# The split of the weights into a rounded and a remaining part, in pieces of 512 instead of 256 elements

## The chip, the cores and the metric

The kernel runs on one core of one Trainium2 chip. The metric is device time in microseconds of one execution: the median of several runs. Of the core's engines this text speaks of PE (TensorE; PEld are its weight loads), DVE (VectorE), ACT (ScalarE), POOL (GpSimd) and SP (SyncE, which issues the DMAs).

## What is computed

One decoder layer for 512 tokens of width 1024, in float32:

```
u = rms_norm(x, norm_pre)
q_a, kv_a, g_a, z_a, qkv_b, z_b, merge = split(u @ w_in)
kc, vc = compress(kv_a[0]), compress(kv_a[1])        # small two-layer nets w1, w2 over blocks of 32
o_a = gated sum of compressed, selected and window attention (8 heads, 2 kv groups)
o_b = block-sparse attention (8 heads), which at 512 tokens is plain causal attention over two blocks of 256
y_a, y_b = o_a * silu(z_a), o_b * silu(z_b)
m = sigmoid(gate_a) * (y_a @ w_a) + sigmoid(gate_b) * (y_b @ w_b)
out = x + rms_norm(m @ w_o, norm_post)
```

All softmaxes carry a distance penalty.

## The kernel before

The matmuls take operands in a rounded 32-bit form (fp32r). To keep float32 precision the kernel writes each operand as a rounded part `hi` and the remaining part `lo`, and multiplies hi by hi, hi by lo and lo by hi (L168 to L170 in `proj`).

**Weights.** They come in 30 chunks of 128 x 2048 elements (1 MB), each loaded by SP into one of two `raw` buffers, then split on the chip in two slots of 1024 columns each; a slot has one of three `ws` buffers, which holds hi and lo. Splitting a slot is a list of pieces, and each piece is two instructions of the method `split_pieces`:

```
act.activation(hi, src, AF.Copy)                     # L115, ACT: the rounded part
dve.tensor_tensor(lo, src, f(hi), op=ALU.subtract)   # L116, DVE: what remains
```

Four functions say how a slot is cut: `std_pieces`, `pair_pieces` and `w1_pieces` cut it into four pieces of 256 elements per partition; `half_pieces(n)` into pieces of n elements, 256 for the chunks vb and 512 for the two chunks wo. So 28 chunks have 2 x 4 pieces of 256 (224 pieces), the last two chunks 2 x 2 pieces of 512 (8 pieces).

**Order.** `stream_gen` runs the chunks one after another: early chunks (kcvc, ksw, w1k, qa0, w1v, qa1), ten chunks that fill the attention phase (za, vb, zb, qkb), twelve of the merge (ga, gb, ab) and wo. While one slot is multiplied, after every step of the projection one piece of the next slot is issued. The last piece of a chunk's second slot calls `load_ahead`, which issues the load of a later chunk into the `raw` buffer that this sets free. In the attention phase `fill` interleaves the projection with the 24 attention units: scores (L928, L929), the addition of the bias with a running minimum on DVE (L932), the exponential on ACT (L934), scaling on DVE and POOL (L946), transposes on PE (L967), the split of the transposed probabilities on ACT (L968) and DVE (L969, which also frees the PSUM buffer for the next transposes), and the product with v (L987, L988).

At the start a block under `tc.manual_schedule()` writes the order out by hand; it holds the eight pieces of the first chunk, kcvc, as `first[0]` to `first[7]`. Behind it the framework's planner, with costs of its own, sets the order in which each engine gets its instructions: they need not stand in the order of the lines. On the chip each engine runs its list in that fixed order and waits at an instruction whose input or buffer is not ready.

The small net of the compression (L770 to L774 on ACT and DVE) is followed by a transpose on PE, `ph_k` or `ph_v` (L781), which stands in PE's list between matmuls of the chunk qa.

Of the kernel before, what the change touches and what calls it, by code (L numbers as in the profile page):

```python
# [41 lines left out]
def hybrid_block(ctx, tc, x, norm_pre, w_in, pe_k, w1_k, w2_k, pe_v, w1_v, w2_v,  # L42
# [21 lines left out]
    def ps(tag, name):  # L64
        return psum.tile([128, 512], F32, tag=tag, name=name)
# [54 lines left out]
    def std_pieces(s):  # L120

        def piece(k0):
            def fn(raw, slot):
                r = raw.rearrange("p (k c) -> p k c", k=8)[:, k0:k0 + 2, s * 128:(s + 1) * 128]
                v = slot.rearrange("p (h k c) -> p h k c", h=2, k=8)
                return r, v[:, 0, k0:k0 + 2], v[:, 1, k0:k0 + 2]
            return fn
        return [piece(k) for k in range(0, 8, 2)]

    def half_pieces(n):  # L130

        kk = 1024 // n
        def pieces(s):
            def piece(k):
                def fn(raw, slot):
                    r = raw.rearrange("p (k c) -> p k c", c=n)[:, s * kk + k]
                    v = slot.rearrange("p (h k c) -> p h k c", h=2, c=n)
                    return r, v[:, 0, k], v[:, 1, k]
                return fn
            return [piece(k) for k in range(kk)]  # L140
        return pieces

    def pair_pieces(s):

        def piece(k0):
            def fn(raw, slot):
                r = raw.rearrange("p (k g c) -> p k g c", k=8, g=2)[:, k0:k0 + 2, :, s * 64:(s + 1) * 64]
                v = slot.rearrange("p (h k g c) -> p h k g c", h=2, k=8, g=2)
                return r, v[:, 0, k0:k0 + 2], v[:, 1, k0:k0 + 2]
            return fn  # L150
        return [piece(k) for k in range(0, 8, 2)]

    def w1_pieces(s):
        def piece(k0):
            def fn(raw, slot):
                r = raw.rearrange("p (l e) -> p l e", l=16)[:, 8 * s + k0:8 * s + k0 + 2]
                v = slot.rearrange("p (l h e) -> p l h e", l=8, h=2)
                return r, v[:, k0:k0 + 2, 0], v[:, k0:k0 + 2, 1]
            return fn
        return [piece(k) for k in range(0, 8, 2)]  # L160

    def proj(slot, dst, kts=range(KT), rh=None, rl=None):

# [281 lines left out]
    def take_pieces(item):  # L445
        c, sl = item
        pieces = c.split_pieces(sl)

        def last(go=pieces[-1]):
            go()  # L450
            unsplit[c.name] -= 1
            if not unsplit[c.name]:
                del unsplit[c.name]
            load_ahead()
        return pieces[:-1] + [last]
# [92 lines left out]
    def x_stats(tt, parts=1):  # L548
        sq = s4.tile([128, D], F32, tag="s4", name=f"sq_{tt}")
        ss = early.tile([128, 2], F32, name=f"ss_{tt}")  # L550
        rs[tt] = early.tile([128, 1], F32, name=f"rs_{tt}")
        w = D // parts
        for n in range(parts):
            act.activation(sq[:, n * w:n * w + w], xt[tt][:, n * w:n * w + w], AF.Square, accum_out=ss[:, n:n + 1])
        sss[tt] = ss
        if parts == 2:
            r = rs[tt]
            dve.tensor_scalar(ss[:, 0:1], ss[:, 0:1], 1.0 / D, EPS, op0=ALU.mult, op1=ALU.add)
            dve.scalar_tensor_tensor(r, ss[:, 1:2], 1.0 / D, ss[:, 0:1], op0=ALU.mult, op1=ALU.add)
            pool.tensor_tensor(r, r, neghalf, op=ALU.pow)  # L560

    def x_stats_r(tt):
        rstd_of(sss[tt][:, 0:1], rs[tt], EPS)
# [3 lines left out]
    def x_diag(tt):  # L567
        diag[tt] = early.tile([128, 128], F32, name=f"diag_{tt}")
        dve.tensor_scalar(diag[tt], ident, rs[tt], None, op0=ALU.mult)

    def x_scale(tt, h):
        c = slice(512 * h, 512 * h + 512)
        act.activation(xt[tt][:, c], xt[tt][:, c], AF.Copy, scale=rs[tt])

    def x_transpose(tt, h):

        pt = ps("to"[h], f"ut_{tt}_{h}")
        for k in range(4):
            kk = 4 * h + k
            o, i = pt[:, k * 128:(k + 1) * 128], xt[tt][:, kk * 128:(kk + 1) * 128]  # L580
            if tt in diag:
                mm(o, i, diag[tt], start=True, stop=True)
            else:
                pe_eng.transpose(o, i, ident)
        up[tt, h] = pt

    def x_hi(tt, h):

        u = xt[tt][:, 512 * h:512 * h + 512].rearrange("p (k t) -> p k t", k=4)
        dve.tensor_tensor(u, up[tt, h].rearrange("p (k t) -> p k t", k=4),  # L590
                          npreT[:, 4 * h:4 * h + 4, None].to_broadcast([128, 4, 128]), op=ALU.mult)
        hi = uh[:, 4 * h:4 * h + 4, tt * 128:tt * 128 + 128]
        up[tt, h] = (u, hi)
        act.activation(hi, u, AF.Copy)

    def x_low(tt, h, eng=dve):
        u, hi = up[tt, h]
        eng.tensor_tensor(ul[:, 4 * h:4 * h + 4, tt * 128:tt * 128 + 128], u, f(hi), op=ALU.subtract)

    def wa_hi(k, eng=None):  # L600
        if eng is not None:
            eng.tensor_copy(wa_hl[:, 0, k:k + 2], ra[:, k:k + 2])
            return
        act.activation(wa_hl[:, 0, k:k + 2], ra[:, k:k + 2], AF.Copy)

    def wa_lo(k, eng=dve):
        eng.tensor_tensor(wa_hl[:, 1, k:k + 2], ra[:, k:k + 2], f(wa_hl[:, 0, k:k + 2]), op=ALU.subtract)
# [4 lines left out]
    def a_mm(tt, parts, last=2, ks=range(KT)):  # L612
        a = slice(tt * 128, tt * 128 + 128)
        if tt not in apt:
            apt[tt] = ps("s", f"pa_{tt}")
        pt = apt[tt]
        for n in parts:
            u, h = ((uh, 0), (ul, 0), (uh, 1))[n]
            for k in ks:
                mm(pt[:, 0:280], u[:, k, a], wa_hl[:, h, k], start=(n == 0 and k == 0),  # L620
                   stop=(n == last and k == KT - 1))
# [16 lines left out]
    first = [p for sl in range(2) for p in take_pieces(order[sl])]  # L638
# [3 lines left out]
    def keep_warm(n):  # L642
        for _ in range(n):
            mm(wt[:, 0:128], ident, ident, start=True, stop=True)

    with tc.manual_schedule():
        keep_warm(10)
        x_stats(0, 2)
        pt = ps("t", "npreT_ps")
        pe_eng.transpose(pt[:, 0:KT], npre, ident[0:KT, 0:KT])  # L650
        x_stats(1)
        x_diag(0)
        x_transpose(0, 0)
        x_stats_r(1)
        dve.tensor_copy(npreT, pt[:, 0:KT])
        wa_hi(0)
        x_transpose(0, 1)
        x_diag(1)
        x_transpose(1, 0)
        wa_hi(2)  # L660
        x_hi(0, 0)
        wa_hi(4, pool)
        wa_hi(6)
        wa_lo(4, pool)
        x_transpose(1, 1)
        x_hi(0, 1)
        x_stats(2)
        a_mm(0, (0,))
        x_hi(1, 0)
        x_low(0, 0)  # L670
        x_low(0, 1)
        x_hi(1, 1)
        x_stats_r(2)
        a_mm(0, (1,))
        wa_lo(0)
        x_stats(3)
        a_mm(1, (0,))
        a_mm(0, (2,), 2, (4, 5, 0, 1))
        x_scale(2, 0)
        x_scale(2, 1)  # L680
        wa_lo(2)
        x_stats_r(3)
        a_mm(1, (2,), 2, (4, 5, 0, 1))
        x_transpose(2, 0)
        wa_lo(6)
        x_scale(3, 1)
        a_mm(0, (2,), 2, (2, 3, 6, 7))
        x_low(1, 1, pool)
        x_low(1, 0)
        x_scale(3, 0)  # L690
        x_transpose(2, 1)
        x_hi(2, 0)
        a_evac_act(0)
        a_mm(1, (2,), 1, (2, 3, 6, 7))
        x_transpose(3, 1)
        x_hi(2, 1)
        x_low(2, 0)
        x_low(2, 1, pool)
        x_transpose(3, 0)
        a_evac_dve(0)  # L700
        a_mm(1, (1,), 1)
        x_hi(3, 0)
        x_hi(3, 1)
        a_evac_act(1)
        a_mm(2, (0,))
        x_low(3, 0)
        a_mm(2, (2,), 1)
        a_mm(2, (1,), 1)
        a_evac_dve(1)
        x_low(3, 1)  # L710
        first[0]()
        a_evac_act(2)
        first[1]()
        first[2]()
        first[3]()
        first[4]()
        first[5]()
        a_mm(3, (0, 1, 2))
        first[6]()
        a_evac_act(3)  # L720
        a_evac_dve(3)
        a_evac_dve(2)
        first[7]()

    early_cm.__exit__(None, None, None)
    early_cm = tc.tile_pool(name="early2", bufs=1)
# [333 lines left out]
    for h in range(2):  # L1060
        raw = wraw.tile([128, 2048], F32, tag="raw", name=f"raw_wo1{h}")
        load_wo(1, h)(raw)
        r = raw.rearrange("p (k c) -> p k c", k=4)
# [4 lines left out]
    for tt in range(NT):  # L1068
# [5 lines left out]
        r = ss[:, 7:8]  # L1074
# [4 lines left out]
        for n, (c0, c1) in enumerate(cuts):  # L1079
            if n == 0:  # L1080
                o = wo0_banks[tt]
            else:
                o = ps(("mm", "o")[(tt + n + 1) % 2], f"wo1_{tt}_{n}")[:, 0:c1 - c0]
                w = slice(c0 - 512, c1 - 512)
# [48 lines left out]
```

## Time and profile before

| | |
|---|---|
| time, median of 3 runs | 472.69 us (472.64 to 472.72) |
| profiled execution, its own time | 473.4 us |
| its span, first to last instruction | 471.6 us (1.8 us lie around it) |
| PE busy | 460.0 us, 98% of the span |
| DVE busy | 325.2 us, 69% |
| ACT busy | 256.1 us, 54% |
| POOL busy | 125.0 us, 27% |
| granted TensorE clock, mean | 0.997 |

Busy time is the union of an engine's instructions. An instruction's duration runs from its start to its end; neighbours on an engine may overlap, so durations may add up to more than busy time. A busy PE is not PE at its peak, because matmuls are pipelined and their ends are modelled.

### The profile page before, as it was taken

How to read it: one execution, taken by the hardware profiler on the slowest of the kernel's cores; microseconds unless marked ns; L12 is line 12 of the kernel's file. 1: busy time of each engine (PE TensorE's matmuls, PEld its weight loads, DVE VectorE, ACT ScalarE, POOL GpSimd, SP SyncE). 2: the span in 40 equal slices, each digit the busy share in tenths (PEclk: the TensorE clock that was granted, in tenths of full speed). 3: DMA queues.
4: the chain of work that ended last, by engine and by line, in shares of the span. 5: the costliest groups of instructions: out<-in, count | busy, mean ns of one | idle time of the engine just before them, and what ended most of it. 6: DMA issues, size and time to landing. Idle time of an engine off the chain costs nothing.

```text
span 471.6 us, 6999 instructions
## 1 busy us (share of the span) xinstructions
PE 460.0 (98%) x2415; PEld 390.9 (83%) x2415; DVE 325.2 (69%) x836; ACT 256.1 (54%) x684; POOL 125.0 (27%) x144
## 2 busy tenths in 40 slices
PE   7999999999999999999999999999999999999994
PEld 7988877888999888888888888887888888888884
DVE  2858867997786878877788987677584264275044
ACT  5854556676565757655675766676433333324021
POOL 6500006423331323323144553433221010020000
PEclk9999999999999999999999999999999999999998
DMA  8633248214032030230220221131225324223133
GB/s 291 174 90 90 68 112 199 70 29 151 0 91 90 1 90 12 79 89 1 90 90 1 90 89 44 48 91 53 83 89 124 113 69 141 91 89 135 44 135 133
DMA packets 45091, 42.08 MB, mean 89 GB/s; under 512 B 1624, under 2 KB 39808, under 8 KB 45056
## 3 DMA queue, kind: packets, MB, share of 16 engines
q1 hardware_dynamic: 44912, 41.12, 29.5%
q10 hardware_dynamic: 144, 0.52, 0.3%
q8 instruction: 19, 0.31, 0.3%
q14 instruction: 16, 0.13, 0.1%
HBM read 39.54 MB, written 2.10 MB: 88 GB/s over the span
## 4 chain that ended last, share of the span: by engine, by line
PE 86%; DVE 5%; ACT 3%; DMA 3%; POOL 1%; issue 1%; SPq 0%; POOLq 0%; DVEq 0%; ACTq 0%
PE t L967 5%; PE mm_ga L168 3%; PE mm_ga L170 3%; PE mm_ga L169 3%; PE s L928 3%; PE mm_gb L169 3%; PE mm_gb L170 3%; PE s L929 3%; PE mm_gb L168 3%; PE o L988 3%; PE mm_qkb L170 3%; PE mm_qkb L169 3%; PE mm_qkb L168 3%; PE o L987 3%; PE pa L620 3%; PE mm_vb L287 2%
## 5 line engine op out<-in xcount | busy, mean ns | idle before, releaser
L934 ACT ACTIVATE p<-p,st 128x512 f32<-128x512 f32 (+3 forms) x96 | 53.1, 555 | 23.5 <-DVE st L932 23.0
L946 POOL TENSOR_SCALAR p<-p,st 128x256 f32<-128x256 f32 (+1 forms) x48 | 44.1, 929 | 64.6 <-DVE st L943 22.9
L968 ACT ACTIVATE pt<-t 128x512 fp32r<-128x512 f32 (+1 forms) x72 | 35.4, 524 | 27.4 <-PE t L967 26.8
L969 DVE TENSOR_TENSOR pt<-t,pt 128x512 fp32r<-128x512 f32 (+1 forms) x72 | 40.8, 594 | 8.2 <-ACT pt L968 7.7
L932 DVE CUSTOM_DVE_ANT_0 p<-s,bias_a 128x512 f32<-128x512 f32 (+3 forms) x64 | 29.1, 485 | 10.5 <-PE s L929 10.4
L967 PE MATMUL t<-ident,p 128*128 128x128 f32 x240 | 34.7, 274 | 1.3 <-DVE pt L969 1.0
L967 PEld LDWEIGHTS t<-ident,p 128*128 128x128 f32 x240 | 27.5, 140 | 6.1 <-DVE pt L969 3.4
L351 POOL TENSOR_TENSOR ga<-ga,gb 128x512 f32<-128x512 f32 x8 | 11.7, 1465 | 77.2 <-DVE gb L350 77.2
L995 POOL TENSOR_TENSOR z<-ot,z 64x512 f32<-64x512 f32 x16 | 20.6, 1287 | 21.7 <-DVE ot L994 21.7
L168 PE MATMUL mm_qkb<-uh,ws_qkb 128*128 128x512 f32 x64 | 25.9, 404 | 0.0
L168 PE MATMUL mm_gb<-uh,ws_gb 128*128 128x512 f32 x64 | 25.6, 400 | 0.0
L168 PE MATMUL mm_ga<-uh,ws_ga 128*128 128x512 f32 x64 | 25.6, 400 | 0.0
L946 DVE TENSOR_SCALAR p<-p,st 128x512 f32<-128x512 f32 (+1 forms) x48 | 25.2, 565 | 0.5
L169 PE MATMUL mm_gb<-ul,ws_gb 128*128 128x512 f32 x64 | 25.4, 397 | 0.0
L170 PE MATMUL mm_gb<-uh,ws_gb 128*128 128x512 f32 x64 | 25.3, 396 | 0.0
L170 PE MATMUL mm_ga<-uh,ws_ga 128*128 128x512 f32 x64 | 25.3, 395 | 0.0
L169 PE MATMUL mm_qkb<-ul,ws_qkb 128*128 128x512 f32 x64 | 25.3, 395 | 0.0
L169 PE MATMUL mm_ga<-ul,ws_ga 128*128 128x512 f32 x64 | 25.3, 395 | 0.0
L170 PE MATMUL mm_qkb<-uh,ws_qkb 128*128 128x512 f32 x64 | 25.3, 395 | 0.0
L116 DVE TENSOR_TENSOR ws_ab<-raw_ab,ws_ab 128x256 fp32r<-128x256 f32 x32 | 12.8, 456 | 16.6 <-ACT ws_ab L115 16.6
L886 POOL TENSOR_SCALAR bias_b<-dbase 128x512 f32<-128x512 f32 x8 | 12.4, 1544 | 38.2 <-DVE st L932 38.2
L886 POOL TENSOR_SCALAR bias_a<-dbase 128x512 f32<-128x512 f32 x8 | 12.1, 1507 | 37.8 <-DVE st L932 33.0
(311 smaller groups left out, 1391.6 us busy)
## 6 DMA issues: line engine op xcount, KB each, us to landing
raw_qkb<-in_w_in_dram SPq DMA_DIRECT2D x8, 512.0 KB, 5.2
raw_ga<-in_w_in_dram SPq DMA_DIRECT2D x4, 1024.0 KB, 5.3
raw_gb<-in_w_in_dram SPq DMA_DIRECT2D x4, 1024.0 KB, 5.1
raw_wo<-in_w_o_dram SPq DMA_DIRECT2D x4, 1024.0 KB, 5.1
raw_qa<-in_w_in_dram SPq DMA_DIRECT2D x4, 512.0 KB, 6.1
raw_za<-in_w_in_dram SPq DMA_DIRECT2D x4, 512.0 KB, 5.3
raw_vb<-in_w_in_dram SPq DMA_DIRECT2D x2, 1024.0 KB, 5.2
raw_zb<-in_w_in_dram SPq DMA_DIRECT2D x2, 1024.0 KB, 5.2
```

The source lines that it names most:

```text
L168: mm(dst, v[:, 0, k], rh(n), start=(n == 0), stop=False)
L169: mm(dst, v[:, 0, k], rl(n), start=False, stop=False)
L170: mm(dst, v[:, 1, k], rh(n), start=False, stop=(n == len(kts) - 1))
L620: mm(pt[:, 0:280], u[:, k, a], wa_hl[:, h, k], start=(n == 0 and k == 0), stop=(n == last and k == KT - 1))
L886: pool.tensor_scalar(t, dbase, slope, None, op0=ALU.mult)
L932: dve.tensor_tensor_reduce(pp, src, bias[:, 384 - 128 * i:512], 1.0, 3.0e38, ALU.add, ALU.min, st[:, 0, i:i + 1])
L934: act.activation(pp, pp, AF.Exp, bias=st[:, 0, i:i + 1], scale=-1.0, accum_out=st[:, 1, i:i + 1])
L946: (dve if i >= 2 else pool).tensor_scalar(pp, pp, st[:, 1, i:i + 1], None, op0=ALU.mult)
L967: pe_eng.transpose(tp[:, b * 128:(b + 1) * 128], p_of(u, i)[:, 128 * j:128 * j + 128], ident)
L968: act.activation(h[:, c0:c0 + n], tp[:, 0:n], AF.Copy)
L969: dve.tensor_tensor(l[:, c0:c0 + n], tp[:, 0:n], f(h[:, c0:c0 + n]), op=ALU.subtract)
L995: pool.tensor_tensor(zs[zt][mine], t[mine], zs[zt][mine], op=ALU.mult)
```

## The change

The four cutting functions give pieces of 512 elements per partition: four rows of 128 (or pairs of 64) at a time instead of two, and in `half_pieces` as many rows of n as make 512. So a slot has two pieces instead of four; for n = 512 nothing changes. In the hand-written block the eight calls `first[0]` to `first[7]` become four: `first[0]` before the evacuation `a_evac_act(2)`, `first[1]` and `first[2]` behind it, and `first[3]` at the end.

```diff
--- before.py
+++ after.py
@@ -121,43 +121,43 @@
 
         def piece(k0):
             def fn(raw, slot):
-                r = raw.rearrange("p (k c) -> p k c", k=8)[:, k0:k0 + 2, s * 128:(s + 1) * 128]
+                r = raw.rearrange("p (k c) -> p k c", k=8)[:, k0:k0 + 4, s * 128:(s + 1) * 128]
                 v = slot.rearrange("p (h k c) -> p h k c", h=2, k=8)
-                return r, v[:, 0, k0:k0 + 2], v[:, 1, k0:k0 + 2]
+                return r, v[:, 0, k0:k0 + 4], v[:, 1, k0:k0 + 4]
             return fn
-        return [piece(k) for k in range(0, 8, 2)]
+        return [piece(k) for k in range(0, 8, 4)]
 
     def half_pieces(n):
 
-        kk = 1024 // n
+        kk, w = 1024 // n, 512 // n
         def pieces(s):
             def piece(k):
                 def fn(raw, slot):
-                    r = raw.rearrange("p (k c) -> p k c", c=n)[:, s * kk + k]
+                    r = raw.rearrange("p (k c) -> p k c", c=n)[:, s * kk + k:s * kk + k + w]
                     v = slot.rearrange("p (h k c) -> p h k c", h=2, c=n)
-                    return r, v[:, 0, k], v[:, 1, k]
+                    return r, v[:, 0, k:k + w], v[:, 1, k:k + w]
                 return fn
-            return [piece(k) for k in range(kk)]
+            return [piece(k) for k in range(0, kk, w)]
         return pieces
 
     def pair_pieces(s):
 
         def piece(k0):
             def fn(raw, slot):
-                r = raw.rearrange("p (k g c) -> p k g c", k=8, g=2)[:, k0:k0 + 2, :, s * 64:(s + 1) * 64]
+                r = raw.rearrange("p (k g c) -> p k g c", k=8, g=2)[:, k0:k0 + 4, :, s * 64:(s + 1) * 64]
                 v = slot.rearrange("p (h k g c) -> p h k g c", h=2, k=8, g=2)
-                return r, v[:, 0, k0:k0 + 2], v[:, 1, k0:k0 + 2]
+                return r, v[:, 0, k0:k0 + 4], v[:, 1, k0:k0 + 4]
             return fn
-        return [piece(k) for k in range(0, 8, 2)]
+        return [piece(k) for k in range(0, 8, 4)]
 
     def w1_pieces(s):
         def piece(k0):
             def fn(raw, slot):
-                r = raw.rearrange("p (l e) -> p l e", l=16)[:, 8 * s + k0:8 * s + k0 + 2]
+                r = raw.rearrange("p (l e) -> p l e", l=16)[:, 8 * s + k0:8 * s + k0 + 4]
                 v = slot.rearrange("p (l h e) -> p l h e", l=8, h=2)
-                return r, v[:, k0:k0 + 2, 0], v[:, k0:k0 + 2, 1]
+                return r, v[:, k0:k0 + 4, 0], v[:, k0:k0 + 4, 1]
             return fn
-        return [piece(k) for k in range(0, 8, 2)]
+        return [piece(k) for k in range(0, 8, 4)]
 
     def proj(slot, dst, kts=range(KT), rh=None, rl=None):
 
@@ -712,15 +712,11 @@
         a_evac_act(2)
         first[1]()
         first[2]()
-        first[3]()
-        first[4]()
-        first[5]()
         a_mm(3, (0, 1, 2))
-        first[6]()
         a_evac_act(3)
         a_evac_dve(3)
         a_evac_dve(2)
-        first[7]()
+        first[3]()
 
     early_cm.__exit__(None, None, None)
     early_cm = tc.tile_pool(name="early2", bufs=1)
```

## Rows read from the trace of the kernel before

**Rows 1.** Page part 1: engine, busy us (share of the span), instructions.

```profile
PE 460.0 (98%) x2415; PEld 390.9 (83%) x2415; DVE 325.2 (69%) x836; ACT 256.1 (54%) x684; POOL 125.0 (27%) x144
```

**Rows 2.** Page part 4, first line: the chain that ended last, by engine.

```profile
PE 86%; DVE 5%; ACT 3%; DMA 3%; POOL 1%; issue 1%; SPq 0%; POOLq 0%; DVEq 0%; ACTq 0%
```

**Rows 3.** Windows from 20 us to the last matmul; columns in the first line.

```profile
core 0: us, PE busy (x) PEld busy (x) DVE busy (x) ACT busy (x) POOL busy (x), PEclk, DMA share, GB/s
...
48.00:78.00 30.00, 28.22 (x138) 22.85 (x137) 21.01 (x52) 16.34 (x46) 5.57 (x10) 1.00 0.52 134
...
130.00:330.00 200.00, 198.86 (x1110) 170.79 (x1109) 160.50 (x453) 131.97 (x364) 70.95 (x64) 1.00 0.22 62
330.00:465.60 135.60, 135.51 (x615) 111.51 (x614) 64.80 (x120) 43.13 (x107) 14.68 (x12) 1.00 0.33 105
sum 445.60, PE 442.38 PEld 373.64 DVE 313.42 ACT 241.65 POOL 112.23; mean PE 88.48 PEld 74.73 DVE 62.68 ACT 48.33 POOL 22.45
```

**Rows 4.** Waits of PE: engine and line <- releaser: us, times, longest.

```profile
PE ph_k L781 <- DVE h_k L774: 1.0, 1, 1.0
PE ph_v L781 <- DVE h_v L774: 0.8, 1, 0.8
```

**Rows 5.** Waits of PE's weight loads, same columns.

```profile
PEld t L967 <- DVE pt L969: 3.4, 7, 1.0
```

**Rows 6.** Line L115 on ACT by tile: duration ns min/median/max, first and last start.

```profile
L115 ACT ACTIVATE ws_qkb<-raw_qkb x32: 400/404/419, 155.4 to 238.2; 128x256 fp32r<-128x256 f32 x32
...
L115 ACT ACTIVATE ws_wo<-raw_wo x8: 615/622/633, 410.9 to 427.3; 128x512 fp32r<-128x512 f32 x8
```

**Rows 7.** Line L116 on DVE by tile, same columns.

```profile
L116 DVE TENSOR_TENSOR ws_qkb<-raw_qkb,ws_qkb x32: 393/417/857, 156.0 to 239.4; 128x256 fp32r<-128x256 f32 x32
...
L116 DVE TENSOR_TENSOR ws_vb<-raw_vb,ws_vb x16: 409/415/532, 103.5 to 128.9; 128x256 fp32r<-128x256 f32 x16
...
L116 DVE TENSOR_TENSOR ws_wo<-raw_wo,ws_wo x8: 679/693/1784, 411.6 to 428.2; 128x512 fp32r<-128x512 f32 x8
```

**Rows 8.** Timeline of ACT, unbroken runs of pieces: start, us, instructions.

```profile
51.16 1.34 ACT L115 ACTIVATE ws_w1k<-raw_w1k 128x256 fp32r<-128x256 f32 x4
...
410.94 1.14 ACT L115 ACTIVATE ws_wo<-raw_wo 128x512 fp32r<-128x512 f32 x2
```

**Rows 9.** Timeline of DVE, unbroken runs of pieces, same columns.

```profile
53.03 1.43 DVE L116 TENSOR_TENSOR ws_w1k<-raw_w1k,ws_w1k 128x256 fp32r<-128x256 f32 x4
...
411.59 1.29 DVE L116 TENSOR_TENSOR ws_wo<-raw_wo,ws_wo 128x512 fp32r<-128x512 f32 x2 [4.38 <-ACT ws_wo L115]
```

**Rows 10.** Timeline of ACT where two loads land, same columns.

```profile
61.05 0.72 ACT L115 ACTIVATE ws_w1v<-raw_w1v 128x256 fp32r<-128x256 f32 x2 [2.99 <-DMA raw_w1v<-in_cmp_w_v_dram]
...
75.97 0.42 ACT L115 ACTIVATE ws_za<-raw_za 128x256 fp32r<-128x256 f32 x1 [2.57 <-DMA raw_za<-in_w_in_dram]
76.30 0.29 ACT L773 ACTIVATE h_v<-h_v 62x128 f32<-62x128 f32 x1
```

**Rows 11.** Chain of 60 to 78 us: by line, and one piece.

```profile
by line: DMA raw_qa<-in_w_in_dram 41.9%; DMA raw_za<-in_w_in_dram 29.4%; ACT ws_qa L115 8.0%; DVE ws_w1v L116 7.4%; ACT ws_w1v L115 5.1%; DVE ws_qa L116 3.8%; ACT q_a L203 3.3%; ACT q_a L204 3.3%; DVE ws_za L116 2.4%; PE mm_qa L168 2.4%; AC
...
70.58 5.29 DMA raw_za<-in_w_in_dram
```

**Rows 12.** Tile raw_w1k: its split and its load, columns as in rows 6.

```profile
L115 ACT ACTIVATE ws_w1k<-raw_w1k x8: 400/404/417, 39.3 to 52.1; 128x256 fp32r<-128x256 f32 x8
...
L270 SPq DMA_DIRECT2D raw_w1k<-in_cmp_w_k_dram x1: 861/861/861, 29.0 to 29.0; - x1
```

**Rows 13.** Chain of 186 to 193 us: start, us, what.

```profile
190.99 0.43 DVE ws_qkb L116
```

**Rows 14.** Chain of 312 to 323 us, same columns.

```profile
317.59 0.34 DVE ws_ab L116
...
319.10 0.76 DVE ws_ab L116 x2
```

**Rows 15.** Windows, a second table: one stretch, columns as in rows 3.

```profile
78.00:104.00 26.00, 26.00 (x133) 21.19 (x132) 25.42 (x78) 18.57 (x50) 10.31 (x13) 1.00 0.17 49
```

## The prediction

> **What bounds the kernel now.** I read the busy times first: PE is busy for 98% of the span [rows 1]. The chain that ended last agrees: 86% of it is PE, 8% DVE and ACT together [rows 2]. So the time is PE's work plus the moments in which PE has none. The windows say where these are: from 20 us to the last matmul at 465.6 us PE is busy 442.38 of 445.60 us, which leaves 3.22 us in all [rows 3]. Of these 1.78 us lie between 48 and 78 us, 1.14 us between 130 and 330 us, and 0.09 us in the last 136 us [rows 3]. The waits name their causes. Two transposes of the compression net, ph_k and ph_v, wait 1.0 and 0.8 us for DVE [rows 4]; in the attention phase PE's weight loads wait seven times, 3.4 us in sum, for the DVE half of the split of the transposed probabilities [rows 5]. (That sum and the windows overlap only in part: an earlier matmul may still count as busy while the next weight load waits.) DVE and ACT matter only where they make PE late.
>
> **What a pair of joined pieces saves.** By durations a piece of 256 takes ACT 404 ns, one of 512 622 ns [rows 6]; DVE 417 and 693 ns [rows 7]. That would be 2 x 404 - 622 = 186 ns and 2 x 417 - 693 = 141 ns for each pair, but neighbours overlap, so the step from one to the next is what counts. On ACT four pieces in a row take 1.34 us, so a step is (1.34 - 0.40) / 3 = 0.31 us; two of 512 take 1.14 us, a step of 1.14 - 0.62 = 0.52 us [rows 6, 8]. A pair saves 2 x 0.31 - 0.52 = 0.10 us. On DVE the steps are (1.43 - 0.42) / 3 = 0.337 us and 1.29 - 0.69 = 0.60 us [rows 7, 9]; a pair saves 0.07 us. With 28 chunks of 8 pieces, 224 pieces become 112: 11 us less on ACT, 8 us less on DVE, spread over the span. The pieces of wo stay. Nearly all of this is hidden: it shortens work of engines that are 54% and 69% busy [rows 1] beside a PE that isn't waiting. From 330 us on, where a good part of the pieces lie, it cannot give more than 0.09 us [rows 3].
>
> The trace has no strided piece of 512, only contiguous ones (wo). The nearest rows say that the pattern costs nothing: ws_qkb, cut from rows of 128, takes 417 ns, ws_vb, contiguous, 415 ns [rows 7]. From below and above I take 0 to 2 ns a piece; at 112 pieces that is 0.2 us of DVE, hidden.
>
> **The start.** In the hand-written block ACT has one piece less ahead of the last evacuation, and the piece left for the end is twice as long, so DVE ends it about 0.69 - 0.42 = 0.27 us later [rows 7]. That sets the raw buffer free and starts the load of w1k from SP, now at 29.0 us; its first split is at 39.3 us [rows 12]. With some 5.3 us from issue to landing, as for raw_za [rows 11], about 5 us remain: hidden. Without that cover it would cost the 0.27 us. The first chunk's slot is split ahead of the last evacuation as before, so PE's first projection isn't later.
>
> **The two waits of the compression net.** Here ACT stands still at a split until a load lands, and the small tanh (L773) that PE waits for stands behind it: raw_w1v lands near 61.05 us after 2.99 us of ACT idle, raw_za near 75.97 us after 2.57 us [rows 10]. Each load is issued when DVE has finished the split that frees its buffer, so shorter splits start loads sooner. For raw_w1v the split ahead is one run of w1k on DVE: 1.43 us now, 1.29 us after [rows 9], so 0.14 us sooner. Behind the landing two pieces of 256 precede the tanh (0.63 us, two steps); one of 512 takes 0.52 us. DVE then has a lo piece of 0.60 us ahead of its own part instead of one of 0.34 us, starting later too, because its hi part ends 0.22 us later; together this eats up what the load won. I take 0 for ph_k, with -0.1 to +0.3 as the ends.
>
> For raw_za the chain from 60 to 78 us holds 8.0% + 5.1% of its 18 us on ACT's splits, 2.4 us or seven to eight pieces, and 7.4% + 3.8% on DVE's, 2.0 us or six pieces [rows 11]. Joined, that is 3.5 pairs x 0.10 + 3 pairs x 0.07 us. It gives 0.55 us, and the load of qa at the head of the chain starts 0.28 us sooner (two DVE runs of 0.14). So raw_za lands about 0.8 us sooner. Against this stand the piece ahead of the tanh, 0.21 us longer (0.52 for 0.31), and the lo piece ahead of DVE's part, 0.26 us longer. Left are 0.3 us less wait for ph_v; ends: 0 and -0.8, the whole wait.
>
> **The waits of the attention phase.** PE's next transposes need a PSUM buffer that DVE's second half (L969) frees. A split piece that stands ahead of L969 on DVE delays it. Near 191 us one piece is in that chain, 0.43 us [rows 13]: if a piece of 512 takes its place, PE waits 0.60 - 0.337 = 0.26 us longer; if the planner puts it behind, 0.34 us less. Near 318 us three are in it, 0.34 + 0.76 = 1.10 us [rows 14]: two pieces of 512 give 1.20 us, one 0.60 us. So a place changes by -0.5 to +0.26 us, whichever way the order falls. Over seven places I take -0.1 us, with +-1 us.
>
> Sum: 0 - 0.3 - 0.1 = -0.4 us. The profiled execution took 473.4 us, 471.6 of span and 1.8 around it, 0.7 us more than the median of the runs shown; against its own time the sum gives 473.0 us, against the median 472.69 - 0.4 = 472.3 us. A measurement of this kernel can tell a change of about 0.2%, 0.95 us, so this forecast is no change.
>
> **Rivals.**
> Faster: the splits' delays are what PE waits for, and they go. For it speaks that each of the named waits has splits in its chain [rows 10, 13, 14]; the most direct way is that the planner puts the tanh ahead of the split that waits for its load, and both waits of the net vanish, 1.78 us [rows 3]: 470.9 us. Against it: both loads still land late, and the order would have to change. The bound is 3.22 us, 469.5 us. The Trainium skill has a rule for it: "VectorE: DVE Perf Modes", section on the TRN2 errata, says that operands in SBUF cost a fixed latency per instruction, and advises tiles of at least 512 elements. By its formula for a tensor_tensor, an estimate is 157 ns saved per joined pair, 17.6 us over 112 pairs, and if DVE set the end, 455 us. The trace has 0.07 us per pair because neighbours overlap, and DVE doesn't set the end.
>
> Slower: a longer piece holds DVE or ACT when an urgent instruction comes. Its place is DVE between 78 and 330 us; between 78 and 104 us DVE is busy 25.42 of 26 us [rows 15], so it has no slack there, and behind each lo piece queue the bias additions (L932) for which ACT's exponentials wait, and L969 for which PE waits. Each place at which a piece of 512 takes the place of one of 256 costs 0.26 us. With four more such places than today the loss can be told, 1 us; with eight, one in every third of the 24 attention units, it is 2.1 us, 474.8 us. For it speaks that a hand-off every unit has little room there; against it that DVE's mean load falls by 8 us.
>
> The change does what it says in any case; that strided pieces of 512 cost more is the only exception, and it would have to cost over 0.07 us each to turn the saving, which the rows don't suggest. I put it with the slower case.
>
> **Chances and range.** Order of events as now, within 0.2%: 0.39, with a range of its own of 471.8 to 473.4 us. Faster: 0.34, 470.9 us at its most direct, 469.5 at most. Slower: 0.27, 474.8 us at eight places. The range 470.4 to 474.7 us leaves out the last part of either.
>
> **What would show it.** L115 and L116 on 512 elements, 112 each besides wo, near 622 and 693 ns; DVE's busy time lower by about 8 us, ACT's by about 11; PE's busy time and its 0.09 us after 330 us unchanged; the waits for ph_k and ph_v still there, near 1.0 and 0.5 us. I am wrong if PE's idle time from 20 us on, now 3.22 us, moves by over 1 us: down at ph_k and ph_v for the faster case, up at L967 waiting for L969 for the slower one. A changed order on PE itself, which I can't read from here, would show as matmuls of a chunk at other places between the units.

## The result, and the profile after

The changed kernel takes 475.73 us (475.45 to 476.19, 4 runs) against 472.71 us (472.64 to 473.31, 4 runs) for the kernel before on the same chip: a ratio of 1.0058, 95% interval [1.0044, 1.0072]. By this ratio it is slower by some 2.7 us (the two medians lie 3.0 us apart), and it lies 1 us above the upper end of the range. Its profiled execution took 476.19 us, 473.9 of them span.

Lines behind L712 stand four lower in the changed kernel: L777 is the transpose of the net, L963 that of the probabilities, L965 its split on DVE. Page part 1 of the changed kernel, to be read against [rows 1]:

```profile
PE 460.2 (97%) x2415; PEld 389.7 (82%) x2415; DVE 321.4 (68%) x724; ACT 246.3 (52%) x572; POOL 130.0 (27%) x144
```

DVE and ACT have 112 instructions less each, and are less busy; PE does the same work in the same busy time. (POOL is 5.0 us busier for the same 144 instructions; why, no run here shows.) The windows say where PE lost its time (columns as in [rows 3]; PEclk is the granted clock):

```profile
48.00:78.00 30.00, 28.18 (x131) 22.93 (x129) 19.69 (x35) 15.15 (x31) 3.73 (x9) 0.94 0.53 136
...
94.00:112.00 18.00, 17.21 (x91) 13.78 (x91) 17.36 (x47) 12.82 (x31) 5.37 (x5) 1.00 0.19 59
130.00:330.00 200.00, 198.87 (x1117) 171.12 (x1116) 159.01 (x409) 128.43 (x320) 73.83 (x66) 1.00 0.21 59
...
63.50:66.50 3.00, 3.00 (x11) 2.50 (x9) 1.29 (x2) 1.75 (x4) 0.00 (x0) 0.50 0.02 5
```

The same stretch between 94 and 112 us in the kernel before:

```profile
94.00:112.00 18.00, 17.79 (x97) 14.77 (x96) 17.55 (x52) 12.87 (x35) 5.19 (x5) 1.00 0.19 59
```

Two things are new: 0.58 us less PE in the window from 94 to 112 us, and a stretch behind 63 us in which PE is busy all the time, but at a granted clock of 0.50, 1.2 GHz. Busy time doesn't show that loss; the mean of 0.94 between 48 and 78 us does. The waits of PE, and of its weight loads, in the changed kernel (columns as in [rows 4]):

```profile
PE ph_k L777 <- DVE h_k L770: 1.8, 1, 1.8
...
PE t L963 <- DVE pt L965: 1.0, 4, 0.3
...
PE t L963 <- DVE pc L873: 0.6, 2, 0.4
PE mm_vb L287 <- DVE v_b L303: 0.3, 1, 0.3
PE ph_v L777 <- DVE h_v L770: 0.2, 1, 0.2
...
PEld t L963 <- DVE pt L965: 3.9, 8, 0.7
```

ph_k waits 1.8 us where 1.0 was before [rows 4], and ph_v only 0.2 where it was 0.8. The wait for v_b (L303) is new. That for pc (L873) has grown; the kernel before has it once:

```profile
PE t L967 <- DVE pc L877: 0.2, 1, 0.2
```

**At ph_k.** ACT and DVE of the changed kernel where raw_w1v lands (start, us, instructions):

```profile
60.65 1.15 ACT L115 ACTIVATE ws_w1v<-raw_w1v 128x512 fp32r<-128x512 f32 x2 [3.11 <-DMA raw_w1v<-in_cmp_w_v_dram]
61.71 0.29 ACT L769 ACTIVATE h_k<-h_k 62x128 f32<-62x128 f32 x1
...
61.31 1.29 DVE L116 TENSOR_TENSOR ws_w1v<-raw_w1v,ws_w1v 128x512 fp32r<-128x512 f32 x2 [1.99 <-ACT ws_w1v L115]
62.52 0.28 DVE L770 SCALAR_TENSOR_TENSOR h_k<-h_k 62x128 f32<-62x128 f32 x1
```

Two pieces of 512 stand ahead of the tanh, the whole slot, not two of 256 as in [rows 10]: the planner put half of the slot ahead before, now all of it. From the landing to the end of the DVE step that PE waits for it is 62.80 - 60.65 = 2.15 us. Before, ACT started at 61.05 us [rows 10] and this row of the old kernel ended at 62.46, 1.41 us:

```profile
62.19 0.27 DVE L774 SCALAR_TENSOR_TENSOR h_k<-h_k 62x128 f32<-62x128 f32 x1
```

So ph_k comes 0.74 us later. PE in the changed kernel behind it:

```profile
62.86 0.27 PE L777 MATMUL ph_k<-ident,h_k 62*128 62x62 f32 x1 [1.82 <-DVE h_k L770]
...
63.95 0.63 PE L170 MATMUL mm_qa<-uh,ws_qa 128*128 128x512 f32 x1
64.37 0.63 PE L168 MATMUL mm_qa<-uh,ws_qa 128*128 128x512 f32 x1
...
67.51 0.39 PE L169 MATMUL mm_qa<-ul,ws_qa 128*128 128x512 f32 x1
67.74 0.40 PE L170 MATMUL mm_qa<-uh,ws_qa 128*128 128x512 f32 x1
```

A matmul starts every 0.42 us near 64 us, and every 0.23 us near 67.5 us: PE had paused, and the granted clock was halved from 63.2 to 66.6 us.

**Between 94 and 112 us.** DVE of the changed kernel:

```profile
95.29 0.68 DVE L116 TENSOR_TENSOR ws_za<-raw_za,ws_za 128x512 fp32r<-128x512 f32 x1
...
96.91 0.68 DVE L116 TENSOR_TENSOR ws_za<-raw_za,ws_za 128x512 fp32r<-128x512 f32 x1
...
98.12 0.68 DVE L873 TENSOR_TENSOR pc<-tc,pc 64x512 fp32r<-64x512 f32 x1
...
100.56 1.05 DVE L942 TENSOR_SCALAR p<-p,st 128x512 f32<-128x512 f32 x2
101.65 0.69 DVE L965 TENSOR_TENSOR pt<-t,pt 128x512 fp32r<-128x512 f32 x1
...
110.27 0.68 DVE L116 TENSOR_TENSOR ws_vb<-raw_vb,ws_vb 128x512 fp32r<-128x512 f32 x1
110.99 0.69 DVE L873 TENSOR_TENSOR pc<-tc,pc 64x512 fp32r<-64x512 f32 x1
```

Three long pieces stand ahead of the splits of pc, which free the PSUM buffer for PE's next transposes. Three transposes come late, two that wait for pc and one that waits for pt (L965):

```profile
100.68 0.63 PE L963 MATMUL t<-ident,p 128*128 128x128 f32 x4 [0.21 <-DVE pc L873]
...
102.39 0.44 PE L963 MATMUL t<-ident,p 128*128 128x128 f32 x2 [0.16 <-DVE pt L965]
...
111.83 0.63 PE L963 MATMUL t<-ident,p 128*128 128x128 f32 x4 [0.42 <-DVE pc L873]
```

The length of the pieces is not all of it. In the kernel before, DVE split pt ahead of the two scalings of p, now behind them (100.56 us above), and only the last of the three transposes waited. Its rows, of DVE and of PE:

```profile
99.06 0.69 DVE L969 TENSOR_TENSOR pt<-t,pt 128x512 fp32r<-128x512 f32 x1
99.67 0.94 DVE L946 TENSOR_SCALAR p<-p,st 128x512 f32<-128x512 f32 x2
...
108.83 0.63 PE L967 MATMUL t<-ident,p 128*128 128x128 f32 x4 [0.21 <-DVE pc L877]
```

Measured as in the table below, PE falls behind by 0.26, 0.38 and 0.21 us at the three; the largest step is the one with the scalings. Leaving the pieces out, the two lists of DVE differ at six instructions of 604, five of them between 96 and 110 us; ACT's and PE's lists differ there too. So the planner, given longer pieces, has put other instructions in another order as well. How much of this loss is length and how much is order, no run here separates in full.

**How far PE is behind.** Gaps of 0.1 to 0.3 us are hard to add up from waits. A plainer measure: take one matmul, its start in both traces, and the difference. The table gives how far PE lies behind the kernel before, in us, at the matmul that started there at the time in the head. Differences at 51.36 us are taken off; they come from the start (-0.71 to +0.34 us in all these traces), which differs from execution to execution (below). 71 us lies behind ph_k, 92 us behind ph_v.

```
512 in                       71 us  92 us 112 us 152 us 192 us 253 us 333 us 454 us
all (changed kernel)         +2.43  +1.74  +2.60  +2.86  +2.71  +3.17  +2.83  +2.83
e1 all, again                +2.28  +1.61  +2.47  +2.73  +2.58  +3.07  +2.72  +2.72
e2 early chunks              +2.42  +1.51  +1.52  +1.53  +1.53  +1.54  +1.53  +1.53
e3 attention chunks          -0.11  +0.39  +1.23  +1.49  +1.34  +1.83  +1.82  +1.82
e4 merge chunks              -0.14  +0.01  +0.03  +0.03  +0.03  +0.05  -0.33  -0.33
e8 none, issued in pairs     -0.05  +0.00  -0.00  +0.00  -0.00  -0.05  -0.09  -0.09
e9 vb1, zb, qkb              -0.24  -0.15  -0.15  +0.09  -0.05  +0.43  +0.43  +0.43
e10 za0, za1, vb0            +0.00  +0.51  +1.38  +1.39  +1.40  +1.40  +1.38  +1.38
e11 all but w1v              +0.28  +0.38  +1.24  +1.47  +1.34  +1.82  +1.45  +1.45
e12 attention, pieces 1024   -0.41  +1.93  +2.10  +2.20  +1.90  +2.45  +2.46  +2.46
e5 none, tanh held ahead     -0.17  -0.05  -0.07  -0.05  -0.06  -0.04  -0.04  -0.04
e6 all, tanh held ahead      +0.04  -0.73  +0.12  +0.38  +0.24  +0.74  +0.39  +0.39
e7 merge, tanh held ahead    -0.36  -0.23  -0.23  -0.23  -0.23  -0.23  -0.58  -0.58
```

### The profile page after: what moved, and what is told of

It is laid out like the page before. It is cut to its first block, busy times and chain, and to the rows that moved or that the text cites. A ratio compares the mean times of both kernels' runs of the same rounds, so it can differ in the third digit from the quotient of the medians.

```text
span 473.9 us, 6771 instructions
## 1 busy us (share of the span) xinstructions
PE 460.2 (97%) x2415; PEld 389.7 (82%) x2415; DVE 321.4 (68%) x724; ACT 246.3 (52%) x572; POOL 130.0 (27%) x144
## 4 chain that ended last, share of the span: by engine, by line
PE 83%; DVE 9%; ACT 3%; DMA 1%; issue 1%; POOL 1%; POOLq 0%; DVEq 0%; ACTq 0%; SPq 0%
PE t L963 5%; PE mm_ga L168 3%; PE mm_ga L170 3%; PE mm_ga L169 3%; PE mm_gb L169 3%; PE mm_gb L168 3%; PE mm_gb L170 3%; PE o L984 3%; PE s L924 3%; PE s L925 3%; PE o L983 3%; PE mm_qkb L169 3%; PE mm_qkb L168 3%; PE mm_qkb L170 3%; PE pa L620 3%; PE wo L1083 2%
## 5 line engine op out<-in xcount | busy, mean ns | idle before, releaser
L942 POOL TENSOR_SCALAR p<-p,st 128x256 f32<-128x256 f32 (+1 forms) x48 | 46.2, 973 | 65.2 <-DVE st L939 36.0
L965 DVE TENSOR_TENSOR pt<-t,pt 128x512 fp32r<-128x512 f32 (+1 forms) x72 | 41.0, 594 | 10.0 <-ACT pt L964 9.5
L963 PE MATMUL t<-ident,p 128*128 128x128 f32 x240 | 34.8, 274 | 1.6 <-DVE pt L965 1.0
L351 POOL TENSOR_TENSOR ga<-ga,gb 128x512 f32<-128x512 f32 x8 | 13.7, 1716 | 75.2 <-DVE gb L350 75.2
L963 PEld LDWEIGHTS t<-ident,p 128*128 128x128 f32 x240 | 27.5, 140 | 7.2 <-DVE pt L965 3.9
L942 DVE TENSOR_SCALAR p<-p,st 128x512 f32<-128x512 f32 (+1 forms) x48 | 26.2, 585 | 0.7
L882 POOL TENSOR_SCALAR bias_a<-dbase 128x512 f32<-128x512 f32 x8 | 13.4, 1669 | 38.2 <-DVE st L928 33.2
L116 DVE TENSOR_TENSOR ws_ab<-raw_ab,ws_ab 128x512 fp32r<-128x512 f32 x16 | 11.5, 755 | 17.2 <-ACT ws_ab L115 17.2
```

The lines of the kernel that those rows point to most:

```text
L882: pool.tensor_scalar(t, dbase, slope, None, op0=ALU.mult)
L942: (dve if i >= 2 else pool).tensor_scalar(pp, pp, st[:, 1, i:i + 1], None, op0=ALU.mult)
L963: pe_eng.transpose(tp[:, b * 128:(b + 1) * 128], p_of(u, i)[:, 128 * j:128 * j + 128], ident)
L965: dve.tensor_tensor(l[:, c0:c0 + n], tp[:, 0:n], f(h[:, c0:c0 + n]), op=ALU.subtract)
```

## Experiments

**Which chunks.** The time is lost at a few places, so the first question is whose pieces are to blame. One switch decides by the chunk's name how it is cut; the hand-written block at the start follows the cut of kcvc. Everything else is as in the two kernels.

```diff
+    WIDE = lambda name: name[:2] in ("za", "vb", "zb", "qk")
+    step = {"k": 4}
...
             res = []
+            step["k"] = 4 if WIDE(self.name) else 2
             for fn in self.pieces(s):
...
-                r = raw.rearrange("p (k c) -> p k c", k=8)[:, k0:k0 + 4, s * 128:(s + 1) * 128]
+                r = raw.rearrange("p (k c) -> p k c", k=8)[:, k0:k0 + n, s * 128:(s + 1) * 128]
```

*e1_all*, the changed kernel again through this switch.

> The changed kernel once more, every engine's instructions in the same order as in its first profile (28 chunks in pieces of 512). Theory of two places (long pieces stand ahead of an urgent instruction at the compression net's tanh, and on DVE between 95 and 112 us): +2.8 to +3.2 us against before, ph_k waits about 1.8 us, and the clock need not fall, since three of the four timed executions had a mean clock of 0.998. Clock theory (the longer pause at ph_k makes TensorE's clock fall, and the 3.4 us at half clock are the loss): the same time, and the clock falls again behind ph_k, with about 1.5 us lost there.

475.62 us (475.46 to 476.12, 5 runs), ratio 1.0058 [1.0046, 1.0070]: the loss repeats. In the profiled execution, the slowest, the clock falls behind ph_k again (mean granted clock 0.992); in the four others the mean is 0.997 to 0.999.

*e2_early*, 512 in kcvc, ksw, w1k, qa0, w1v and qa1 alone.

> Only the six early chunks (kcvc, ksw, w1k, qa0, w1v, qa1) in pieces of 512, all others in 256. Two places: ph_k waits near 1.8 us as after the change, the wait for ph_v falls by a part of it, so +0.5 to +1.2 us. Clock theory: most of the 3 us is here, +2 us or more, with a fall of the clock in the profile. Spread theory (every longer piece costs a little wherever it stands): 48 of 224 pieces, so 0.21 of 3 us, +0.6 us.

473.92 us (12 runs), 1.0018 [1.0008, 1.0028]; its runs spread from 473.12 to 474.98. The profiled one, the slowest, has the pause at ph_k and the halved clock behind it (+2.42 in the table), gets 0.9 us of it back at ph_v, and nothing changes after.

```profile
PE ph_k L796 <- DVE h_k L789: 1.8, 1, 1.8
```

and its window behind that pause:

```profile
63.80:66.80 3.00, 3.00 (x10) 2.44 (x9) 1.41 (x3) 1.48 (x3) 0.00 (x0) 0.50 0.04 9
```

*e3_fill*, 512 in za, vb, zb and qkb alone.

> Only the ten chunks that fill the attention phase (za, vb, zb, qkb) in pieces of 512. Two places: the second place is here, transposes wait for DVE between 95 and 145 us, +0.8 to +1.5 us. Clock theory: no long pause, so within 0.5 us of before. Spread theory: 80 of 224 pieces, +1.1 us.

474.93 us (474.69 to 475.53, 5 runs), 1.0042 [1.0030, 1.0054], 2.0 us and so more than I expected. These ten chunks hold most of the loss: +0.50 at ph_v, +0.84 to 112 us, +0.26 to 152 us, -0.15 to 192 us, +0.49 to 253 us, nothing after. Its waits:

```profile
PE ph_v L796 <- DVE h_v L789: 1.3, 1, 1.3
...
PE t L982 <- DVE pc L892: 0.6, 2, 0.4
...
PE mm_vb L296 <- DVE v_b L312: 0.3, 1, 0.3
```

*e4_merge*, 512 in ga, gb and ab alone.

> Only the twelve chunks ga, gb, ab in pieces of 512. Two places and clock theory: nothing, within 0.5 us of before, since PE hardly waits from 240 us on. Spread theory: 96 of 224 pieces, +1.3 us.

472.74 us (11 runs), 0.9992 [0.9984, 1.0001]. PE gains 0.38 us between 253 and 333 us, where [rows 14] showed three pieces ahead of L969; the weight loads' waits for that line go from 3.4 us in seven [rows 5] to this:

```profile
PEld t L982 <- DVE pt L984: 2.8, 6, 0.8
```

In the profiled executions the parts add up: 1.53 + 1.82 - 0.33 = 3.02 us, against 2.83 for all together. By the ratios they are 0.85 + 1.99 - 0.38 = 2.46 us, and 0.5 us more lie outside the span (below), against 2.7.

*e8_paired_256*: the pieces stay at 256, but two of them are issued at each step of a projection, as one of 512 is. This keeps the coarser issue and leaves the longer instruction out.

```diff
+            if len(res) == 4:
+                res = [lambda a=a, b=b: (a(), b()) for a, b in (res[0:2], res[2:4])]
             return res
```

> Pieces of 256 as before, but two of them are issued at each step of the projection, as the changed kernel issues 512 elements at a time; the hand-written block as in the changed kernel. If the length of one instruction is what costs: within 0.5 us of before. If it is the coarser issue, two steps a slot instead of four: +2 us or more.

472.92 us (11 runs), 0.9999 [0.9990, 1.0008]: the coarser issue costs nothing. It takes the longer instruction; whether that costs by its time on the engine or by the order that the planner makes for it, this run doesn't tell, since here the order of all other instructions on DVE, ACT and PE is that of the kernel before.

**Whose places.** e3's loss, cut in two by chunks.

*e9_fill_late* and *e10_fill_first*:

> Pieces of 512 only for the last seven of the ten chunks that fill the attention phase (vb1, zb, qkb); everything else stays at 256. Theory of the places (a longer piece stands ahead of an urgent instruction, and each place has its price): the losses seen near ph_v and at 95 to 112 us belong to za and vb0 and must be absent; those near 142 us (+0.25 us) and 224 to 245 us (+0.47 us) and the gain at 195 us (-0.12 us) must be there: +0.6 us against the kernel before, ratio about 1.0013. Rival, the loss is spread over all chunks in proportion: seven tenths of the 2.0 us, +1.4 us, ratio 1.003.

> Pieces of 512 only for the first three chunks of the attention phase (za0, za1, vb0); everything else stays at 256. Theory of the places: +0.48 us at ph_v and +0.85 us at 95 to 112 us, in sum +1.3 us, ratio about 1.0028, nothing behind 130 us. Rival, the loss is spread in proportion: three tenths of 2.0 us, +0.6 us, ratio 1.0013.

e9: 473.52 us (473.06 to 474.41, 11 runs), 1.0015 [1.0007, 1.0024]. e10: 474.61 us (474.09 to 476.00, 6 runs), 1.0036 [1.0024, 1.0049]. The three first chunks cost more than the seven later ones, and each loss sits where its own chunk's pieces are: e10 has +0.51 at ph_v and +0.87 to 112 us and is flat after, e9 has +0.24 to 152, -0.14, +0.48 to 253 us. In the table 0.43 + 1.38 = 1.81 us, e3 has 1.82. A loss in proportion to the pieces is refuted. In e9 the lists of ACT and PE without the pieces are those of the kernel before, and DVE's differs in one instruction, near 226 us: there the steps of +0.25 us at 140 us and +0.17 us at 242 us belong to the longer pieces themselves.

**Longer still.** *e12_fill_1024* (in the switch `step["k"] = 8`, a slot in one piece).

> The ten chunks of the attention phase in pieces of 1024 elements, a whole slot at once; everything else at 256. Theory of the places: a piece takes some 1.15 us on DVE instead of 0.60 (512) and 0.337 (256), so a place where it stands ahead of an urgent instruction costs 0.8 us instead of 0.26: about three times the 2.0 us of pieces of 512 if the order stays as it is, less where the planner moves the piece away; I expect +3.5 to +6 us, ratio 1.0075 to 1.0125. Rival, what costs is the planner's other order and not the length: the loss needn't grow, +1 to +3 us. Rival, fewer instructions help: below the +2.0 us of pieces of 512.

476.17 us (475.99 to 476.32, 5 runs), 1.0066 [1.0054, 1.0078], 3.1 us: below the size that I expected, at the upper end of the rival that blames the order. The loss didn't grow at every place. At ph_v it did: the wait goes 0.8 us [rows 4], 1.3 (e3), 1.8. But between 92 and 112 us it is 0.17 us instead of 0.84: the planner put one of za's long pieces at 83.89 us, away from the splits of pc:

```profile
83.89 1.22 DVE L120 TENSOR_TENSOR ws_za<-raw_za,ws_za 128x1024 fp32r<-128x1024 f32 x1
```

The two transposes that waited for pc lose nothing against the kernel before; the one that waits for pt, behind the scalings as in e3, loses the same 0.38 us as with pieces of 512. So the length sets the price where a piece stands ahead of an urgent instruction, and the planner's order sets which places there are and, as far as this step tells, has a price of its own. And behind the pause at ph_v, another transpose than in e2, the clock falls too (its wait, then the window behind it):

```profile
PE ph_v L796 <- DVE h_v L789: 1.8, 1, 1.8
```

```profile
79.70:82.90 3.20, 3.20 (x9) 2.44 (x8) 1.83 (x6) 2.24 (x3) 1.34 (x3) 0.50 0.68 190
```

**w1v alone.** *e11_all_but_w1v*: everything in 512 except the chunk behind the pause at ph_k.

> The changed kernel with chunk w1v alone back in pieces of 256; three of them now stand ahead of the tanh, not two of 512. Theory: PE's pause at ph_k is some 1.2 to 1.4 us instead of 1.8 to 2.0 us, the granted clock stays at 1.0 there, and the early chunks cost nothing: 475.6 - 0.8 = 474.8 us, ratio 1.004. Rival, the early loss isn't that of w1v's pieces, or the clock falls behind the shorter pause too: 475.6 us, ratio 1.0058. It also has 6771 + 8 instructions: if the time outside the span goes with nearly all chunks being joined, it stays near 2.3 us; if it needs every one of them, it is 1.8 us.

475.11 us (474.37 to 475.78, 6 runs), 1.0045 [1.0033, 1.0057]. Three pieces of 256 stand ahead of the tanh, the wait at ph_k is 1.2 us, the clock stays at 1.00, and at 92 us PE is behind by 0.38 us instead of 1.74. The early loss is w1v's in the trace. The times alone tell less: the intervals of e1 and e11 overlap. Its wait and its window:

```profile
PE ph_k L796 <- DVE h_k L789: 1.2, 1, 1.2
```

```profile
48.00:78.00 30.00, 27.82 (x136) 22.52 (x135) 20.92 (x41) 15.89 (x35) 5.82 (x10) 1.00 0.55 140
```

**Tanh ahead of the splits.** What if both waits of the net go? The first slot's pieces of w1v and za0 are held behind the tanh and the DVE step after it; this is the faster rival's mechanism, for pieces of 256 (e5), of 512 (e6), and with 512 in the merge chunks only (e7). `tail` holds the two instructions of the net.

```diff
+                    with ExitStack() as held:
+                        if s == 0 and self.name in ("w1v", "za0"):
+                            for ins in tail["k" if self.name == "w1v" else "v"]:
+                                held.enter_context(tc.issue_after(ins.ins))
                         act.activation(hi, src, AF.Copy)
                         dve.tensor_tensor(lo, src, f(hi), op=ALU.subtract)
...
-        act.activation(h1, h0, AF.Tanh, scale=0.5)
-        dve.scalar_tensor_tensor(h0, h1, 1.0, h0, op0=ALU.add, op1=ALU.mult)
+        tail[kv] = (act.activation(h1, h0, AF.Tanh, scale=0.5),
+                    dve.scalar_tensor_tensor(h0, h1, 1.0, h0, op0=ALU.add, op1=ALU.mult))
```

> The kernel before, all pieces of 256, with one thing held: on ACT and DVE the pieces of the slots w1v 0 and za0 0 come behind the net's tanh and the step after it, so PE's transposes ph_k and ph_v no longer wait for a load. If ACT's standing at a load is what these waits are: both gone, -1.5 to -1.8 us. Rival (PE would only meet its next wait: the splits of w1v and za0 now end later, and the matmuls that need them wait): within 0.5 us of before.

> The changed kernel, all pieces of 512, with the same two slots held behind the tanh. Two places: the loss at ph_k and the fall of the clock behind it go, what remains against before is DVE between 95 and 245 us, +1.3 us, less the waits that before has too, 1.8 us: -0.8 to +0.3 us against before, and 2.3 to 3.5 us faster than the changed kernel. Rival as in the run with 256: less than 1 us faster than the changed kernel.

> The two slots held behind the tanh, and only the chunks ga, gb, ab in pieces of 512. If both add up: -1.6 to -2.3 us against before, the fastest so far. If the pieces of 512 in the merge bring nothing: as the run with 256.

e5: 472.68 us (11 runs), 0.9994 [0.9985, 1.0002], no gain. The waits at ph_k and ph_v are gone from its list, and two others stand there, behind the late loads of za (sc) and qa (mm_qa):

```profile
PE sc L861 <- DVE q_a L219: 0.9, 1, 0.9
PE mm_qa L182 <- ACT ws_qa L124: 0.6, 1, 0.6
```

e6: 474.08 us (11 runs), 1.0022 [1.0013, 1.0031]. With pieces of 512 the same order takes 1.5 us off the changed kernel (475.62 to 474.08), less than I expected: no long pause, no fall of the clock; the losses from 92 us on stay. Up to 92 us PE even stands 0.73 us ahead of the kernel before, where e5 has 0.05: the wait of sc is gone too. e7: 472.42 us (472.12 to 473.15, 11 runs), 0.9987 [0.9978, 0.9995], less than the sum that I expected, but the lowest median of this study, 0.6 us below the kernel before; its interval overlaps those of e4 and e5.

## Why the prediction was wrong

The forecast was "no change" (-0.4 us); what came is in the main the slower rival, at 475.7 us instead of the 474.8 that I gave for eight places (itself 0.1 us outside the range that I stated). Three terms of the sum failed, and where the clock didn't fall, the attention phase by the most.

**Right.** PE bounds the kernel: DVE and ACT got less busy, and the time grew. A joined piece costs what was forecast: medians of 618 to 642 ns on ACT and 678 to 693 ns on DVE in the changed kernel's rows of L115 and L116, strided or not. Two in a row take 1.15 and 1.29 us as read from wo [rows 8, 9]. The start stayed hidden: in the changed kernel SP issues the load of w1k at 28.70 us, and ACT's first split of it, at 39.01 us, follows the instruction before it without a wait.

**The sign of being wrong** that I named, PE's idle time from 20 us on moving by over 1 us, would have missed the loss: up to the last matmul at 467.8 us PE is busy 443.89 of 447.80 us, so its idle time went from 3.22 to 3.91 us. Time at half the clock counts as busy.

**ACT and DVE savings.** ACT saved 9.8 us of the 11, DVE 3.8 of 8. A part may be that DVE's other instructions took 2.9 us longer in sum; I haven't separated it, and it decided nothing.

**ph_k, taken as 0 with an upper end of +0.3: the step that failed first.** I let one piece of 512 take the place of two of 256 ahead of the tanh. The planner put two there, so the landing is followed by 0.74 us more, and PE's idle time ahead of ph_k rose from 0.96 to 1.82 us. I had no row for the planner's choice and should have carried "the whole slot" as the end. A second cost I had not priced at all: in the profiled execution the clock fell behind that pause, which makes up the rest of the +2.43 us, 2.43 - 0.86 = 1.57 us. 0.69 us come back at ph_v, because the load that ph_v waits for goes on meanwhile. The fall is not what the medians show: it lasts 3.4 us, which alone takes 0.0036 off the mean granted clock of a span, and in seven of the nine executions of the changed kernel and e1 the mean is 0.997 or more. Those have the loss without such a fall.

**ph_v, taken as -0.3.** Its own price was right: I had 0.21 + 0.26 = 0.47 us for the longer piece on ACT and DVE, e3 has +0.50. What failed is the gain set against it, raw_za 0.8 us sooner. In e11, where the clock stays at 1.00, ACT's starts on w1v and za lie 75.23 - 60.47 = 14.76 us apart, against 75.97 - 61.05 = 14.92 us [rows 10]: 0.16 us. But e11 leaves w1v, half of the splits in that chain [rows 11], in pieces of 256. With the tanh held ahead the gain did come: at 92 us e6 stands 0.73 - 0.05 = 0.68 us ahead of e5. In the changed kernel's own profile the fall of the clock lies in between, so what it kept of the gain stays open.

**The attention phase, taken as -0.1 with +-1.** e3 has +1.43 us from 92 us on. The price of 0.26 us a place was not exceeded where nearly all other instructions kept their order: +0.25 us at 140 us (the wait for v_b), +0.20 and +0.17 us at 222 and 242 us. The +0.84 to 112 us is no check of it: its largest step, 0.38 us, goes with the scalings of p that the planner put ahead of L965. It shows little at the place that I named: the weight loads' waits for L969, now L965, went from 3.4 us [rows 5] to 3.9. What failed is the sign: I let the order of pieces fall either way, and there were six steps more (0.26, 0.38, 0.21, 0.25, 0.20, 0.17 us) and one small gain. That the planner would move other instructions was not in the sum at all. [Rows 15] was the row to weigh: at 25.42 of 26 us DVE had no slack there, and saving 0.07 us a pair couldn't make any. Where DVE had slack, in the merge, the gain that I worked out from [rows 14] did come: -0.38 us (e4), within the -0.5 to +0.26 forecast.

**The faster rival** needs more than its order: with pieces of 256 (e5) the next wait takes the place of the one removed. With pieces of 512 (e6) 0.73 us of its 1.78 came up to 92 us, and the attention phase took more than that back (+1.47 us up to 253 us).

**The rule of the Trainium skill** ("VectorE: DVE Perf Modes", section on the TRN2 errata: a fixed latency for each instruction on SBUF, hence tiles of at least 512 elements) is not borne out as a gain here. With 112 pairs joined DVE was busy 3.8 us less, and the kernel was 2.7 us slower.

**Still open: 0.5 us outside the span.** Time minus span is 2.23 to 2.35 us in all 20 runs of the three kernels with every chunk in 512 (the changed one, e1, e6; 6771 instructions), and 1.73 to 1.86 us in all 83 runs of the other kernels but e11. e11, with 6779 instructions, has both: 1.84 to 1.87 us in three runs, 2.15, 2.36 and 2.38 in three. So some 0.5 us of the loss isn't in the trace. That it goes with the program's length near this count is a guess from these numbers. On the pages one thing goes with it: the queue q14, of kind instruction, has 14 packets in these three kernels and in e11, and 16 or 17 in all others. It doesn't decide alone, since e11's profiled execution, with 14, is one with 1.86 us.

## What to carry to other kernels

When instructions on an engine without slack are made longer, count the places where one of them stands ahead of an instruction that the bounding engine waits for: the price is up to the whole extra length each time (here 0.17 to 0.25 of 0.26 us), and the saving in total busy time doesn't pay it back. The same edit can be right in one phase and wrong in another, so try it by phase (here: the merge alone was neutral; with the tanh held ahead, 0.13% faster). Where a planner sets the order, bound an edit by the worst order that it may choose, not by the one that it chose before, and compare the order of the other instructions before you put a loss down to the ones you changed.

## What the runs showed of the hardware

- A pause of PE of under 2 us can cost more than itself. In the four profiles in which PE waited 1.7 or 1.8 us at a transpose (the changed kernel, e1 and e2 at ph_k, e12 at ph_v), the granted clock fell to 0.50 within 1.1 us of the end of the wait and stayed there for over 3 us, and 1.3 to 1.6 us were lost besides the longer pause (in the changed kernel 1.57, in e12 1.93 + 0.41 - 1.0 = 1.34). In the profiles with waits of 0.2 to 1.4 us there it stayed at 1.00. It isn't so in each execution of the changed kernel: its other three runs have a mean granted clock of 0.998 (0.995 in the profiled one) and spans of 473.2, 473.2 and 473.7 us, 0.2 to 0.7 us shorter than the profiled 473.9. Nor is a wait of 1.4 us shown to be safe: one execution of e10 that was not profiled took 476.00 us at a mean of 0.993, where the profiled one took 474.33 at 0.999.
- The clock rises to 1.00 for the first time at 5.2 us in the changed kernel's trace and at 11.0 us in that of the kernel before. In the three traces in which it rises late (the kernel before, e3, e12: 11.0 to 11.3 us) PE's start at 51.36 us lies at 0.00 to +0.34 us, in the others (5.2 to 7.3 us) at -0.71 to +0.01 us. That is a spread of up to 1 us, as much as many of the effects here; hence the table takes it off.
